# T's products behind Gram's, and the layer change's first transposes within the last products

## The chip, the cores and the metric

The kernel runs on one core of a Trainium2 chip. The metric is the device time of one execution in microseconds (us); lower is better. Times of several executions are given by their median. TensorE (PE) multiplies, VectorE (DVE) and ScalarE (ACT) work element by element, GpSimd (POOL) does the same and issues DMAs, SyncE (SP) issues DMAs.

## The reference

Two residual layers over 512 positions of 2048 channels. The first is gated differential attention with 8 heads, the second is gated RWKV-7 time mixing with 32 heads of 64 channels, whose state follows a generalised delta rule. Cut to what matters:

```python
x = x + out                                   # each layer: x <- x + W_out( mixer(rms_norm(x)) * silu(gate) )

# layer 0, per head: two softmaxes over 128 channels each, subtracted, times v
a = p[:, :, 0] - lam * p[:, :, 1]
o = rms_norm(a @ v, subln_w) * (1.0 - lambda_init) * silu(gate)

# layer 1: p = h @ w_in, mixed with the position before, split into r, k, v, g, dw, da
def step(S, inp):
    r_t, w_t, k_t, v_t, a_t, b_t = inp        # a = -kk, b = kk * iclr, kk = normalised k
    sa = jnp.einsum('bhvk,bhk->bhv', S, a_t)
    S = S * w_t[:, :, None, :] + sa[..., None] * b_t[:, :, None, :] + v_t[..., None] * k_t[:, :, None, :]
    y = jnp.einsum('bhvk,bhk->bhv', S, r_t)
    return S, y
```

## The kernel before

**Products and precision.** Each float32 operand is split into a rounded high part and the rest (`split_w` for weights: a copy on ScalarE, a subtraction on VectorE), and `mm3` (L114) makes three products of them. Nearly all products have 512 columns. `tick` counts these products: the kernel weaves small dependent work into the large products by hand. A `Chain` is a generator whose steps are issued on TensorE behind the large product at which its count of products runs out; each `yield n` asks for n more products before the next step. Only the first chain in the list counts down. `finish` issues what is left at once. Within this, the order of each engine's queue is fixed when the program is built, from priorities and modelled readiness; on the chip each queue runs in that order.

**Layer 0, attention.** While the large projections of head h run, a chain does the attention of head h - 1, in 4 blocks of rows: `scores`, `turn` (transposes of the weights a), `weigh` (product with v), and `turn_y` (L395: transposes of the result y into yT). `turn_y` uses PSUM tag pa, which has two banks and which `scores` uses too; `turn` uses pb, which has one. One pass of the loop is 40 products long, 21 for the last head, and between the first `yield 8` and the last one the block's weighing and scores are issued.

**Layer 0, end, and the change of layers.** The output product's second half of columns is done by `seven`, a scheme with seven products of blocks in place of eight. Its last part is product "22", summed into the banks z (tag pa) in three rounds of 12 products and added to x by `take("21", z)`. Behind `seven` stands the normalisation for layer 1: the sums of squares give rs for the first and the second 256 rows (rsqrt by 11 small steps on VectorE), `scale` multiplies x (L771), `half_h` transposes two column blocks of one half of the rows (L805, tag pa), `make_h` splits them into hH and hL, and the products named lora (L114) use these at once: 12 products of 256 columns for each pair of column blocks.

**Layer 1, the pairs.** 16 pairs of heads, j = 0 to 15. An iteration j has the large projections v of j, k of j + 1, the gate of j - 3, and r of j + 1, 48 products each (the gate from j = 3 on). Behind the 18th product of v the function `behind` is called:

- `gram` (L1065): 32 products of AR and BK of pair j into 4 banks gp; before the copies of their result (L1072) it takes one step of the chain of pair j - 1 (`before.step`). Then come the two sums (L984, L985), and the result is written to DRAM as ltd (L1084, on ScalarE's queue).
- `t_solve`: LT is loaded from ltd (L1118, POOL's queue), VectorE solves 31 dependent steps (L1129, L1131), and the result Tm goes to DRAM as td (L1133).
- `group_norm` of pair j - 2.

The chain of pair j - 1 is made at the start of iteration j, and its first step is taken there. In `t_combine` this step brings T in from td (L1146, SP's queue, four DMAs) and transposes it (L1155, T1, two transposes on VectorE, queued behind `g.centred`, the end of the centring of the pair before). After GAP_D products come T's first products (L1161, px, 32 small ones) with four copies (L1164, L1167); after GAP_X more its second ones (L1171) with two copies (L1174); after GAP_T more the scan: 8 chunks with three small dependent products each (L1242, L1253, L1260), 6, 6 and 8 products apart. At its end come the outputs Y (L1282, L1286) and their centring (L1297 to L1299).

With GAP_D = 18 the first products are issued at the 18th product of v by `tick`, just ahead of `behind`; the step that `gram` then takes is that of the second products. AR is made by `stage2` (L1049) at the start of iteration j on VectorE; r, from which it is made, is mixed there just before (L898).

Of the kernel before, what the change touches and what calls it, by code (L numbers as in the profile page):

```python
# [13 lines left out]
F32 = mybir.dt.float32  # L14
# [9 lines left out]
P = 128  # L24
# [3 lines left out]
NT = T // P  # L28
# [304 lines left out]
def attention(g, h, qkT, qkL, sq, V, VL, G, gap, rows=None):  # L333


    nc, w = g.nc, g.work
    yT = w.tile([P, 2, T], F32, name="yTh", tag="yTh", bufs=1)
    blocks = [Ctx() for _ in range(NT)]

    def scores(t):  # L340
        b, N = blocks[t], (t + 1) * P
        mx = g.small.tile([P, 2], F32, name="mx", tag="mx")
        nb = g.small.tile([P, 2], F32, name="nb", tag="nb")
        sm = g.small.tile([P, 2], F32, name="sm", tag="sm")
        pr = []
        for c in range(2):
            s = g.ps.tile([P, 512], F32, name="sc", tag="pa", bufs=2)
            ts = slice(t * P, (t + 1) * P)
            mm3(nc, s[:, :N], qkT[:, c, ts], qkL[:, c, ts], qkT[:, 2 + c, 0:N], qkL[:, 2 + c, 0:N], True, True)
            nc.vector.tensor_tensor_reduce(  # L350
                out=s[:, :N], in0=s[:, :N], in1=g.mask[:, (NT - 1 - t) * P :], scale=1.0, scalar=NEG,
                op0=ALU.add, op1=ALU.max, accum_out=mx[:, c : c + 1])
            nc.vector.scalar_tensor_tensor(nb[:, c : c + 1], mx[:, c : c + 1], -1.0, sq[:, t, c : c + 1],
                                           ALU.mult, ALU.mult)
            p_ = w.tile([P, 512], F32, name=f"p{c}", tag=f"p{c}", bufs=2)
            nc.scalar.activation(p_[:, :N], s[:, :N], AF.Exp, bias=nb[:, c : c + 1],
                                 scale=sq[:, t, c : c + 1], accum_out=sm[:, c : c + 1])
            pr.append(p_)
        b.r = g.small.tile([P, 2], F32, name="r", tag="r")
        nc.vector.reciprocal(b.r[:], sm[:])  # L360
        rho = g.small.tile([P, 1], F32, name="rho", tag="rho")
        nc.vector.scalar_tensor_tensor(rho[:], sm[:, 0:1], b.r[:, 1:2], g.neglam[:], ALU.mult, ALU.mult)
        b.a = w.tile([P, 512], F32, name="a", tag="a", bufs=2)
        nc.vector.scalar_tensor_tensor(b.a[:, :N], pr[1][:, :N], rho[:], pr[0][:, :N], ALU.mult, ALU.add)

    def turn(t):
        b, N = blocks[t], (t + 1) * P
        pt = g.ps.tile([P, 512], F32, name="pt", tag="pb")
        for i in range(t + 1):
# [4 lines left out]
        nc.vector.tensor_sub(b.al[:, :N], pt[:, :N], b.at[:, :N].bitcast(F32))  # L374

    def weigh(t):
        b = blocks[t]
        o = g.ps.tile([P, 512], F32, name="o", tag="pc")
        for i in range(t + 1):
            bs = slice(i * P, (i + 1) * P)  # L380
            mm3(nc, o[:, :256], b.at[:, bs], b.al[:, bs], V[:, i, :], VL[:, i, :], i == 0, i == t)
        junk = w.tile([P, 256], F32, name="junko", tag="junko", bufs=2)
        so = g.small.tile([P, 1], F32, name="so", tag="so")
        nc.scalar.activation(junk[:], o[:, :256], AF.Square, scale=b.r[:, 0:1], accum_out=so[:])
        nc.vector.tensor_scalar(so[:], so[:], 1.0 / 256, EPS, ALU.mult, ALU.add)
        ro = g.small.tile([P, 1], F32, name="ro", tag="ro")
# [3 lines left out]
        nc.vector.scalar_tensor_tensor(b.y[:], o[:, :256], ro[:], G[:, t, :], ALU.mult, ALU.mult)  # L390

    def turn_y(t):
        pt = g.ps.tile([P, 512], F32, name="yt", tag="pa", bufs=2)
        for i in range(2):
            nc.tensor.transpose(pt[:, i * P : (i + 1) * P], blocks[t].y[:, i * P : (i + 1) * P], g.ident[:])  # L395
        nc.scalar.copy(yT[:, :, t * P : (t + 1) * P], pt[:, :256].rearrange("p (c q) -> p c q", c=2))

    for i in range(NT + 3):
        if 0 < i <= NT:
            turn(i - 1)  # L400
        if i > 2:
            turn_y(i - 3)
        if i == NT + 2:
            break
        yield 8
        if 1 < i < NT + 2:
            weigh(i - 2)
        if i < NT:
            scores(i)
        yield gap - 8  # L410
    if rows is None:
        nc.scalar.dma_start(out=g.yd[h * 256 : (h + 1) * 256, :].rearrange("(c p) t -> p c t", p=P), in_=yT[:])
    else:
        rows += [split_row(g, yT[:, c, :]) for c in range(2)]
# [71 lines left out]
                          accum_op=ALU.add)  # L486


def seven(g, w, load, rows, sums, c1, c2, acc, Ts, banks, done):

# [35 lines left out]
    last = N - 1  # L526
# [36 lines left out]
    done("22")  # L563
    take("21", X)
    for i in range(N):
        prod(z, i, "22", Ts[i], i == 0, i == last)
    take("21", z)
    done("21")
# [16 lines left out]
def flat(t):  # L585

    n = "abc"[: len(t.shape) - 1]
    n = " ".join(n)
    return t[:].rearrange(f"p {n} -> p ({n})").rearrange("p (k c) -> p k c", k=KG)


def layer0(g, aps):
# [86 lines left out]
    with ExitStack() as cx:  # L679
# [50 lines left out]
        sums = []  # L730
# [27 lines left out]
        def banks(i):  # L758
            if i < 2:
# [6 lines left out]
        seven(g, aps["da_w_out"][0], load, rows, sums, 1024, 1536, acc, [flat(g.C), flat(g.S), T2], banks, done)  # L766

        rs = g.work.tile([P, NT], F32, name="rs1", tag="rs1", bufs=1)
        ss = g.work.tile([P, NT], F32, name="ss1", tag="ss1", bufs=1)
        def scale(cb, t):  # L770
            nc.vector.tensor_scalar(xs[cb][:, t, :], xs[cb][:, t, :], rs[:, t : t + 1], None, ALU.mult)  # L771

        for half in (slice(0, 2), slice(2, 4)):
            with tc.high_priority(offset=SOLVE if half.start else 0):
                nc.vector.reduce_sum(ss[:, half], g.ssx[:, half], AX.X)
                nc.vector.tensor_scalar(ss[:, half], ss[:, half], 1.0 / D, EPS, ALU.mult, ALU.add)
                rsqrt(g, rs[:, half], ss[:, half], 2, "r4")
                if half.start == 0:
                    for cb in range(4):
                        for t in range(2):  # L780
                            scale(cb, t)

        def more_h(n, m):
            for k in range(len(g.hH), min(n, KT)):
# [7 lines left out]
                with tc.high_priority(offset=AHEAD):  # L792
                    make_h(g, ps, KT + k)

        def half_h(k, half, m):

            ps = g.ps.tile([P, 512], F32, name="xT", tag="pa", bufs=2)
            for i in range(2):
                xq, c0 = xs[(k + i) // 4], (k + i) % 4 * P
                for t in range(2):  # L800
                    tt, at = 2 * half + t, (2 * i + t) * P
                    if c0 == 0 and half:
                        scale((k + i) // 4, tt)
                    with tc.issue_after(m.ins) if m else ExitStack():
                        nc.tensor.transpose(ps[:, at : at + P], xq[:, tt, c0 : c0 + P], g.ident[:])  # L805
            for i in range(2):
                with tc.high_priority(offset=AHEAD):
                    make_h(g, ps[:, 256 * i : 256 * i + 256], KT + k + i, k + i, half)

        pts = [g.ps.tile([P, 512], F32, name="lora", tag=tag) for tag in ("pb", "pc")]  # L810
        lora = [(aps["rw_w_in"][0], 4 * D, 2 * RK)]

# [5 lines left out]
            return m  # L818


        m, wts = None, []
# [312 lines left out]
    return ld.ins  # L1134


GAP_D, GAP_X, GAP_T = 18, 19, 8


def t_combine(g, j, p):  # L1140
# [370 lines left out]
```

## Time and profile before

| | |
|---|---|
| three timed runs | 2208.28, 2211.53, 2221.82 us, median 2211.53 |
| the profiled execution | 2206.95 us, span 2205.2 us, mean granted TensorE clock 0.993 |
| TensorE busy | 2171.5 us, 98% |
| VectorE, ScalarE, POOL busy | 1445.4, 1041.9 and 293.8 us |
| layer 0 | about 0 to 1000 us |
| layer 1 | about 1000 to 2205 us; one full iteration takes about 62 us |

A row of the timeline has the start in us from the span's start, the time in us (of several instructions together, if a count over 1 stands at its end), engine, line of the kernel, operation, the tiles written and read, and, in square brackets, how long the engine was idle before it and what ended that. A matmul's printed time includes its way through the array; the next one starts before it ends. The granted clock is a share of TensorE's full speed.

### The profile page before, as it was taken

To read this page: it belongs to the slowest core of one execution; us is meant where nothing else is said; L and a number is where in the kernel's file an instruction comes from. 1 tells how busy PE (TensorE), PEld (TensorE's weight loads), DVE (VectorE), ACT (ScalarE), POOL (GpSimd) and SP (SyncE) were. 2 spreads that over 40 slices of the span, in tenths; PEclk is the share of its full clock that TensorE was granted. 3 is DMA by queue.
4 is the path that set the end of the run, shared out by engine and by line. 5 is a ranking of instruction groups with operands and counts; after the bars stand their busy time and mean duration, and the time that the engine had idled before them with its cause. 6 is when DMAs were issued, how large, how long until landed. Compare 5 with 4: busy or idle time off the path is not lost.

```text
span 2205.2 us, 34098 instructions
## 1 busy us (share of the span) xinstructions
PE 2171.5 (98%) x12260; PEld 1767.9 (80%) x12260; DVE 1445.4 (66%) x3780; ACT 1041.9 (47%) x2118; POOL 293.8 (13%) x637
## 2 busy tenths in 40 slices
PE   9999999999999999999999999999999999999999
PEld 7888888888888888878777787878887788877887
DVE  5664646455654666475667877777778877767644
ACT  5443434334443454345455555555555556545322
POOL 0000000000000000110222222222222222221001
PEclk9999999999999999999999999999999999999999
DMA  6223222222323356653422333333333333446555
GB/s 192 96 79 98 84 96 96 86 96 87 96 77 99 131 171 225 158 117 90 106 57 76 81 87 86 93 97 92 91 87 85 96 91 77 113 123 187 172 167 119
DMA packets 296313, 240.20 MB, mean 109 GB/s; under 512 B 47792, under 2 KB 255680, under 8 KB 296144
## 3 DMA queue, kind: packets, MB, share of 16 engines
q1 hardware_dynamic: 256912, 190.13, 29.3%
q0 software_dynamic: 12384, 29.72, 6.3%
q10 hardware_dynamic: 26848, 18.18, 2.7%
q8 instruction: 96, 1.57, 0.3%
q14 instruction: 73, 0.60, 0.1%
HBM read 217.98 MB, written 19.99 MB: 108 GB/s over the span
## 4 chain that ended last, share of the span: by engine, by line
PE 70%; DVE 19%; issue 4%; DMA 3%; ACT 2%; SPq 0%; POOL 0%; ACTq 0%; DVEq 0%; POOLq 0%
PE pp L114 52%; PE pt L114 5%; DVE wl L103 3%; DVE tmpl L1129 3%; DVE Tm L1131 2%; DMA td<-Tm 2%; DVE VS L1264 1%; PE gp L1065 1%; PE sm L1242 1%; PE lora L114 1%; PE sc L114 1%; PE sm L1260 1%; DMA TT<-td 1%; ACT wh L102 1%; PE sm L1253 1%
## 5 line engine op out<-in xcount | busy, mean ns | idle before, releaser
L103 DVE TENSOR_TENSOR wl<-wraw,wh 128x1024 fp32r<-128x1024 f32 (+2 forms) x319 | 388.9, 1219 | 431.5 <-ACT wh L102 419.0
L102 ACT CAST wh<-wraw 128x1024 fp32r<-128x1024 f32 (+2 forms) x319 | 333.5, 1046 | 513.0 <-PE pp L114 378.3
L114 PE MATMUL pp<-wh,hH 128*128 128x512 f32 x1268 | 499.3, 394 | 0.3 <-DVE gs L326 0.2
L114 PE MATMUL pp<-wh,hL 128*128 128x512 f32 x1268 | 497.7, 393 | 0.1
L114 PE MATMUL pp<-wl,hH 128*128 128x512 f32 x1268 | 497.4, 392 | 0.0
L114 PE MATMUL pp<-hH,wl 128*128 128x512 f32 x1024 | 416.1, 406 | 0.3 <-DVE wl L103 0.3
L114 PE MATMUL pp<-hL,wh 128*128 128x512 f32 x1024 | 415.9, 406 | 0.0
L114 PE MATMUL pp<-hH,wh 128*128 128x512 f32 x1024 | 413.1, 403 | 0.0
L114 PEld LDWEIGHTS pp<-wh,hH 128*128 128x128 f32 x1268 | 238.3, 188 | 48.4 <-PE pp L114 0.6
L114 PEld LDWEIGHTS pp<-wh,hL 128*128 128x128 f32 x1268 | 238.3, 188 | 48.4 <-DVE hL L858 0.5
L114 PEld LDWEIGHTS pp<-wl,hH 128*128 128x128 f32 x1268 | 238.4, 188 | 46.4
L114 PEld LDWEIGHTS pp<-hH,wh 128*128 128x128 f32 x1024 | 194.6, 190 | 36.1 <-issue 0.9
L114 PEld LDWEIGHTS pp<-hL,wh 128*128 128x128 f32 x1024 | 194.6, 190 | 34.9
L114 PEld LDWEIGHTS pp<-hH,wl 128*128 128x128 f32 x1024 | 194.7, 190 | 32.9 <-DVE wl L103 0.7
L1129 DVE SCALAR_TENSOR_TENSOR tmpl<-LT,Tm 128x60 f32<-128x60 f32 (+24 forms) x496 | 135.1, 272 | 10.9
L1248 POOL COPY SA<-VS 64x64 f32<-64x64 f32 x224 | 60.9, 272 | 457.0 <-DVE VS L1264 350.0
L459 POOL DMA_DIRECT2D frow<-yd x12 | 8.9, 746 | 796.4 <-DVE rs_i L63 676.8
L1131 DVE TENSOR_TENSOR Tm<-Tm,tmpl 128x60 f32<-128x60 f32 (+24 forms) x496 | 104.0, 210 | 11.2
L1255 ACT COPY VS<-sm 64x64 f32<-64x64 f32 x256 | 52.9, 207 | 65.8 <-PE sm L1253 61.1
L1245 ACT COPY rhs<-sm 64x64 f32<-64x64 f32 x256 | 52.7, 206 | 53.7 <-PE sm L1242 51.3
L1264 DVE SCALAR_TENSOR_TENSOR VS<-sm,gam,Sg 64x64 f32<-64x64 f32 x192 | 54.1, 282 | 24.7 <-PE sm L1260 20.6
L1251 POOL TENSOR_SCALAR Sg<-SA,gam 128x64 f32<-128x64 f32 x96 | 63.3, 660 | 9.5 <-POOL SA L1248 0.2
(333 smaller groups left out, 3189.6 us busy)
## 6 DMA issues: line engine op xcount, KB each, us to landing
wraw<-in_rw_w_in_dram SPq DMA_DIRECT2D x128, 512.0 KB
wraw<-in_da_w_in_dram SPq DMA_DIRECT2D x254, 256.0 KB
wraw<-in_da_w_out_dram SPq DMA_DIRECT2D x26, 512.0 KB
wraw<-in_rw_w_out_dram SPq DMA_DIRECT2D x26, 512.0 KB
LT<-ltd POOLq DMA_DIRECT2D x64, 132.0 KB, 2.9
yr<-yd SPq DMA_DIRECT2D x28, 256.0 KB
frow<-yd POOLq DMA_DIRECT2D x12, 512.0 KB, 6.9
xq<-in_x_dram SPq DMA_DIRECT2D x16, 256.0 KB
```

The source lines that it names most:

```text
L102: nc.scalar.copy(hi[:, ks], raw[:, ks])
L103: nc.vector.tensor_sub(lo[:, ks], raw[:, ks], hi[:, ks].bitcast(F32))
L114: m = nc.tensor.matmul(out, a, b, start=s, stop=e, skip_group_check=skip)
L1065: m = nc.tensor.matmul(gp[h][:, i * P : (i + 1) * P], BK[r_, c0 + i, :, :], p.AR[r_, c0 + i, :, :], start=True, stop=True)
L1129: nc.vector.scalar_tensor_tensor(tt, LT[:, i : i + 1, i + 1 :].to_broadcast([P, s, n]), n2[:, i : i + 1], Tm[:, 0:s, i : i + 1].to_broadca ...
L1131: nc.vector.tensor_add(Tm[:, 0:s, i + 1 :], Tm[:, 0:s, i + 1 :], tt)
L1242: nc.tensor.matmul(sm[:, 0:P], both(p.G[:, c, 0]), both(VS[:, c]), start=True, stop=True)
L1245: nc.scalar.copy(rhs[r_, :], sm[r_, h * C : h * C + C])
L1248: nc.gpsimd.tensor_copy(p.SA[r_, c - 1, :], VS[r_, c, h, :])
L1251: nc.gpsimd.tensor_scalar(Sg[:], p.SA[:, c - 1, :], p.gam[:, c : c + 1], None, ALU.mult)
L1255: nc.scalar.copy(VS[r_, c, h, :], sm[r_, P : P + C])
L1264: g.state = nc.vector.scalar_tensor_tensor(VS[r_, c + 1, h, :], s_, p.gam[r_, c : c + 1], Sg[r_, :], ALU.mult, ALU.add)
```

## The change

It has three parts.

1. In `attention`, `turn_y` is issued 8 products later, behind `weigh` and ahead of `scores`, and takes bank pb in place of pa. The last block's `turn_y` stays at its place.
2. In the layer change, a new function `begin` is called by `seven` ahead of the last of the three rounds of product "22". It holds the normalisation of the first 256 rows, their first two scales, the transposes of the first four column blocks (two `half_h`, into banks of pool pp) with their `make_h`, and then the other six scales. The loop behind `seven` goes on from there.
3. In `t_combine`, GAP_D goes from 18 to 20 and GAP_X from 19 to 10. At the 18th product of v the first products' count is not yet out, so the step that `gram` takes is now that of the first products, and the second ones follow 10 products later.

```diff
     def turn_y(t):
-        pt = g.ps.tile([P, 512], F32, name="yt", tag="pa", bufs=2)
+        pt = g.ps.tile([P, 512], F32, name="yt", tag="pb")
...
         if 0 < i <= NT:
             turn(i - 1)
+        if i == NT + 2:
+            turn_y(i - 3)
+            break
+        yield 8
+        if i > 1:
+            weigh(i - 2)
         if i > 2:
             turn_y(i - 3)
-        if i == NT + 2:
-            break
-        yield 8
-        if 1 < i < NT + 2:
-            weigh(i - 2)
         if i < NT:
             scores(i)
         yield gap - 8
...
     for i in range(N):
+        if i == last and begin:
+            begin(g.m)
         prod(z, i, "22", Ts[i], i == 0, i == last)
     take("21", z)
...
+        def begin(m):
+            normalise(slice(0, 2))
+            for k in (0, 2):
+                half_h(k, 0, m, (g.pp, "pp", 4))
+            for cb in range(1, 4):
+                for t in range(2):
+                    scale(cb, t)
+
+        seven(g, aps["da_w_out"][0], load, rows, sums, 1024, 1536, acc, [flat(g.C), flat(g.S), T2], banks, done, begin)
+        normalise(slice(2, 4))
...
         for i, (k, half) in enumerate(turns):
-            if i == 0:
-                half_h(k, half, m)
-            if i + 1 < len(turns):
+            if 0 < i < len(turns) - 1:
                 half_h(*turns[i + 1], m)
-            else:
+            elif i:
                 more_h(KT // 2 + 1, m)
...
-GAP_D, GAP_X, GAP_T = 18, 19, 8
+GAP_D, GAP_X, GAP_T = 20, 10, 8
```

More of the change, by code (lines that the diff above doesn't have):

```diff
@@ L486, in add_w, with seven @@
                           accum_op=ALU.add)
-def seven(g, w, load, rows, sums, c1, c2, acc, Ts, banks, done):
+def seven(g, w, load, rows, sums, c1, c2, acc, Ts, banks, done, begin=None):
     nc = g.nc
@@ L765, in layer0 @@
                                               (g.work, "G", 1), (g.wraw, "wraw", 3)))
-        seven(g, aps["da_w_out"][0], load, rows, sums, 1024, 1536, acc, [flat(g.C), flat(g.S), T2], banks, done)
         rs = g.work.tile([P, NT], F32, name="rs1", tag="rs1", bufs=1)
@@ L771, in scale, with normalise @@
             nc.vector.tensor_scalar(xs[cb][:, t, :], xs[cb][:, t, :], rs[:, t : t + 1], None, ALU.mult)
-        for half in (slice(0, 2), slice(2, 4)):
+        def normalise(half):
             with tc.high_priority(offset=SOLVE if half.start else 0):
@@ L778, in layer0 @@
                 if half.start == 0:
-                    for cb in range(4):
-                        for t in range(2):
-                            scale(cb, t)
+                    for t in range(2):
+                        scale(0, t)
         def more_h(n, m):
@@ L793, in more_h, with half_h @@
                     make_h(g, ps, KT + k)
-        def half_h(k, half, m):
-            ps = g.ps.tile([P, 512], F32, name="xT", tag="pa", bufs=2)
+        def half_h(k, half, m, bank=(g.ps, "pa", 2)):
+            ps = bank[0].tile([P, 512], F32, name="xT", tag=bank[1], bufs=bank[2])
             for i in range(2):
@@ L808, in half_h @@
                     make_h(g, ps[:, 256 * i : 256 * i + 256], KT + k + i, k + i, half)
+        def begin(m):
[3 more added lines that the diff above has]
+            for cb in range(1, 4):
+                for t in range(2):
+                    scale(cb, t)
+        seven(g, aps["da_w_out"][0], load, rows, sums, 1024, 1536, acc, [flat(g.C), flat(g.S), T2], banks, done, begin)
+        normalise(slice(2, 4))
         pts = [g.ps.tile([P, 512], F32, name="lora", tag=tag) for tag in ("pb", "pc")]
@@ L818, in products @@
             return m
-        m, wts = None, []
+        m, wts = g.m, []
         turns = [(k, half) for half in range(2) for k in range(0, KT // 2, 2)]
         for i, (k, half) in enumerate(turns):
-            if i == 0:
-                half_h(k, half, m)
-            if i + 1 < len(turns):
+            if 0 < i < len(turns) - 1:
                 half_h(*turns[i + 1], m)
-            else:
+            elif i:
                 more_h(KT // 2 + 1, m)
```

## The prediction

> **What bounds the kernel now.** I read the page first, for the busy engine; then the waits of TensorE, for what still stops it; then, around each place that the diff touches, the timeline of the engines and the granted clock by stretches.
>
> ```profile
> span 2205.2 us, 34098 instructions
> PE 2171.5 (98%) x12260; PEld 1767.9 (80%) x12260; DVE 1445.4 (66%) x3780; ACT 1041.9 (47%) x2118; POOL 293.8 (13%) x637
> ...
> PE px L1161 <- DVE T L1155: 12.5, 13, 3.1
> ...
> PE yt L395 <- DVE y L390: 1.5, 8, 0.3
> ...
> PE lora L114 <- ACT hH L857: 1.1, 1, 1.1
> ```
>
> TensorE (PE) is busy 98% of the span. The columns of a wait are the time in all, how often, and the longest. The change takes no arithmetic away, so it can only win where TensorE stands still, and the three waits shown are those that its three parts touch: T's first products (px, L1161), the transposes of y (yt, L395) and the first products of the second layer (lora). The same question asked of 1260 to 1940 us alone, where the pairs of heads run at full pace, shows how little of the first is left there:
>
> ```profile
> PE px L1161 <- DVE T L1155: 3.2, 7, 1.0
> ```
>
> Of the 12.5 us, 7.8 us are thus outside, mostly in the first three chains, where T is late for another reason (below).
>
> **Second layer, T's products.** Here is TensorE around a pair whose T was in time, and around one whose T was late:
>
> ```profile
> 1391.66 1.09 PE L1161 MATMUL px<-T,G 32*32 32x32 f32 x32
> 1392.68 2.06 PE L1065 MATMUL gp<-AR,BK 64*128 64x128 f32 x32
> 1394.67 1.09 PE L1171 MATMUL px<-TT,X 32*32 32x32 f32 x32
> 1395.69 0.40 PE L984 MATMUL pt<-sHx,ones 128*2 128x512 f32 x1
> 1395.93 0.40 PE L985 MATMUL pt<-sLx,ones 128*2 128x512 f32 x1
> ...
> 1452.87 0.69 PE L1161 MATMUL px<-T,G 32*32 32x32 f32 x16
> 1453.92 0.69 PE L1161 MATMUL px<-T,G 32*32 32x32 f32 x16 [0.36 <-DVE T L1155]
> 1457.55 0.40 PE L984 MATMUL pt<-sHx,ones 128*2 128x512 f32 x1
> ```
>
> A product of 512 columns takes 0.23 to 0.24 us from start to start (1395.69 to 1395.93), and the kernel's gaps count such products. The order is T's first products (1.0 us), Gram (2.0), T's second products (1.0). In time, the group takes 1395.69 - 1391.66 = 4.03 us; with T late it takes 1457.55 - 1452.87 = 4.68. So a wait printed as 0.36 costs 0.65: 0.29 is hidden in the modelled end of the matmul before. The seven waits of 3.2 us are worth 3.2 + 7 x 0.29 = 5.2 us, which is all that the steady pairs can give.
>
> Why is T late? VectorE's queue for the late pair:
>
> ```profile
> 1447.45 0.75 DVE L1299 TENSOR_TENSOR yc<-Y,s 128x256 f32<-128x256 f32 x2
> 1449.62 1.23 DVE L103 TENSOR_TENSOR wl<-wraw,wh 128x1024 fp32r<-128x1024 f32 x1 [1.43 <-ACT wh L102]
> 1450.77 0.74 DVE L898 SCALAR_TENSOR_TENSOR mixr<-pp,prmin_rw_mu_dram,mixr 128x511 f32<-128x511 f32 x1
> 1452.38 0.44 DVE L1155 STREAM_TRANSPOSE T<-TT 64x256 f32<-64x256 f32 x1 [0.87 <-DMA TT<-td]
> 1452.75 0.64 DVE L1049 TENSOR_TENSOR AR<-mixr,E 128x512 f32<-128x512 f32 x1
> 1453.43 0.44 DVE L1155 STREAM_TRANSPOSE T<-TT 64x256 f32<-64x256 f32 x1
> ```
>
> The first transpose of T waits for the DMA that brings TT, and AR, which Gram reads, stands behind it. AR ends at 1453.39, 0.52 us after the group began. **This is the point on which the change turns**: Gram is first now, and if that queue stayed as it is, Gram would wait for AR where T's products waited before: it would begin near 1453.45, and 4.03 us on is 1457.48 instead of 1457.55. That bound is a gain of 0.1 us a pair, next to nothing.
>
> But the queue does not stay as it is, since T itself comes earlier. The Gram values leave through ScalarE and a chain of DMAs before the next T can be solved:
>
> ```profile
> 1394.42 2.06 ACT L1072 COPY G<-gp 128x512 f32<-128x512 f32 x4
> ...
> 1402.12 0.31 ACTq L1084 DMA_DIRECT2D ltd<-G  x1
> ```
>
> Gram began at 1392.68 and its copies started only at 1394.42, after T's own copies. With Gram first it begins 1.0 us earlier, and its first half can be copied after 1.0 us, while ScalarE still has nothing from T to copy: the copies move from 2.8 us after the group's start (1394.42 - 1391.66) to some 1.0, thus 1.8 us earlier. ScalarE's last issue of ltd (1402.12) stands in its queue behind the copies of the scan, and POOL's loads of LT behind that. The scan begins ten products (2.3 us) later, so these issues get ahead of it: 2 to 4 us earlier for LT, and so for T, of the next pair, against a lateness of about 1 us. The second T products, ten products on, no longer stand directly behind Gram: they start 3.0 + 0.5 (the two sums) + 2.3 = 5.8 us after Gram's start. Gram's copies would end at 1.0 + 2.06 and T's four copies, which fill 1392.75 (the end of px) to 1394.42, need 1.7 more: 4.8 us, in time. The scan ends ten products later too: Y's centring (L1297 to L1299), behind which T's transposes are queued, would be ready 2.3 us later; VectorE has the 1.43 us of idle time before wl to take it up, and an earlier end of the solve in front of it. Issued instructions and DMAs stay the same in number; on SP the four TT loads keep their place, and the weight loads behind them wait less if td comes earlier. From 0.1 x 7 = 0.7 to 5.2 us I take **4.0**, nearer the upper end, because the shift (2 to 4 us) is larger than the lateness.
>
> The last pair in this order is a case of its own:
>
> ```profile
> 1946.32 0.69 PE L1161 MATMUL px<-T,G 32*32 32x32 f32 x16 [0.46 <-DVE T L1155]
> 1947.67 0.48 PE L1065 MATMUL gp<-AR,BK 64*128 64x128 f32 x2 [0.67 <-DVE AR L1049]
> ...
> 1940.00:1960.00 20.00, 18.86 (x151) 0.83 0.33 88
> ...
> 1148.83 0.69 PE L1161 MATMUL px<-T,G 32*32 32x32 f32 x16 [1.83 <-DVE T L1155]
> ...
> 1140.00:1160.00 20.00, 18.16 (x139) 0.77 0.28 58
> ...
> 1700.17 0.69 PE L1161 MATMUL px<-T,G 32*32 32x32 f32 x16 [0.97 <-DVE T L1155]
> ...
> 1700.00:1720.00 20.00, 19.33 (x172) 1.00 0.45 115
> ```
>
> (In a row by stretches, the clock stands behind the count.) Here 1.13 us of idle time, among small products, were followed by a lower clock: (1 - 0.83) x 20 = 3.4 us lost. The same follows the 1.83 us at 1148.83 (0.77), and not the 0.97 us at 1700.17. With T in time the idle time goes and, I think, the low clock with it: 0 to 1.1 + 3.4 = 4.5; I take **4.0**. [...]
>
> The first three chains (1148.83 is one) get little: T's products were placed well after Gram there, since T came later still. Zero, with ±3 us for the phase of their clock. The last chain gains by place: its start moves 10 + 2 products (2.8 us) later while its T does not.
>
> ```profile
> 2013.38 0.69 PE L1161 MATMUL px<-T,G 32*32 32x32 f32 x16 [0.43 <-DVE T L1155]
> ...
> 2015.09 0.69 PE L1161 MATMUL px<-T,G 32*32 32x32 f32 x16 [0.58 <-DVE T L1155]
> ```
>
> That is 0 to 1.0; I take **1.0**.
>
> **Layer change.** Before, the first transposes wait until the last sum has left its two banks:
>
> ```profile
> 979.44 0.39 PE L114 MATMUL z<-wh,hL 128*128 128x512 f32 x1
> 980.00 1.25 PE L805 MATMUL xT<-ident,xq 128*128 128x128 f32 x8 [0.18 <-DVE xq L523]
> 982.34 0.47 PE L114 MATMUL lora<-hH,wh 128*96 128x256 f32 x2 [1.08 <-ACT hH L857]
> 984.78 0.60 PE L805 MATMUL xT<-ident,xq 128*128 128x128 f32 x4
> 985.13 0.36 PE L114 MATMUL lora<-hH,wh 128*96 128x256 f32 x1
> ...
> 985.60 0.48 DVE L771 TENSOR_SCALAR xq<-xq,rs 128x512 f32<-128x512 f32 x1
> ```
>
> From the end of z's issue (979.67) to the next four transposes (984.78) pass 5.1 us. The work in it is 8 transposes at 0.09 (four take 984.78 to 985.13) and 12 products of 256 columns at half of 0.23, together 2.1 us, 2.3 with a little for the changeover. So 2.8 us are idle. The change puts the transposes before z's last 12 products, into banks of another pool: the sum's way out, hH and hL are then covered by 12 x 0.23 = 2.8 us of products. What is late next is the second half's scale: ready at 985.60 + 0.48, or 6.4 us after z; it will be wanted after 36 products and 8 transposes, 4.9 us after z, and the hL subtractions that stand between its small steps now are done before. That leaves 0 to 1.5 us late; I count 0.3 of it. Bounds 0 (the cover fails) to 2.8; I take **2.5**. If scale or hL were late before z's last products, TensorE would wait there instead; the first half's scales follow sums that left long before z's.
>
> **First layer, y.** The transposes of y move 8 products and one weighing later, and into bank pb.
>
> ```profile
> 258.50 0.68 DVE L374 TENSOR_TENSOR al<-pt,at 128x512 fp32r<-128x512 f32 x1
> ...
> 260.05 0.28 PE L114 MATMUL o<-V,al 128*128 128x256 f32 x1
> ...
> 268.90 0.44 PE L395 MATMUL yt<-ident,y 128*128 128x128 f32 x2 [0.17 <-DVE y L390]
> ```
>
> 1.8 us more (8 x 0.23) hides waits of 0.17 here and at most 0.3 (the row of waits above). Bank pb is free in time: al, its last reader, ends at 259.18, and the weighing ends at 260.17. The last transposes of a head stay where they were. Of 1.5 us printed plus hidden tails of about 0.15 each, I take **2.0** (bounds: a loss of 1 if pb blocks, a gain of 2.5).
>
> **Sum.** 4.0 + 4.0 + 1.0 + 2.5 + 2.0 = 13.5, less 2.0 for new small waits (AR behind T in a few pairs, X's copies): 11.5 us. The profiled execution took 2206.95 us, its span 2205.2, so it would become 2195.5. The three timed runs before have a median of 2211.53, 4.6 above it, and such a median is what will be read: 2211.5 - 11.5 = **2200 us**. One per cent is 22 us, about what a measurement of this kernel can tell from no change; this is half of it.
>
> **Rivals.**
> 1. *The wait moves to AR.* VectorE's queue keeps T before AR, T gains nothing, Gram waits. For: that order in the rows of 1452. Against: the copies are freed 1.8 us earlier. Steady pairs 0.7, last pair 0; left are 1.0 + 2.5 + 2.0: 2211.5 - 6 = 2205. Chance 0.2.
> 2. *Slower: both transposes of T get ahead of AR.* The scan's ten products push the centring, T's transposes follow it, and AR comes behind both. In the pair of 1452, T from 1452.38, twice 0.44 and AR's 0.64 end at 1453.9: Gram begins 1.05 us late, the group ends at 1457.95, 0.4 later than now. Over 11 pairs that is 5 us. It decides when Gram's idle time passes the 1.13 us that were followed by a low clock in the last pair: 3.4 us in every second of 11 pairs is 19 more. 2211.5 + 24 - 5.5 = 2230; with every fourth, 2220. I put it at 2224. Chance 0.1.
> 3. *The low clock of the last pair stays*, being due to the small products and not to the idle time: 2200 + 3.4 = 2203. [...] Chance 0.1.
> 4. *The layer change does not do what it says*: the transposes wait before the last products for their scale. Its 2.5 us are lost: 2203. For: scale and hL share VectorE with the last wl. Against: the first scales ran well ahead of z's end. Chance 0.1.
>
> **How the numbers follow.** Forecast 0.5, rivals 0.2, 0.1, 0.1 and 0.1. The likeliest case reaches from 2191 (all upper bounds and no dip) to 2208; rivals 1, 3 and 4 lie in it. To take in the unknown phase of the first three chains' clock and the edge of rival 2, the range goes up to 2216. Faster by over 1% (below 2189.4) needs the dips of the first chains to vanish as well: 0.06. Slower by over 1% (above 2233.6) is rival 2 at its worst: 0.05. Within 1%: 0.89.
>
> **What would show it.** Right: Gram's 32 products first, T's 32 behind them without a wait, a group of 3.0 us up to the sums; Gram's copies begin about 1 us after Gram; the waits of px on T fall from 12.5 to near 8, all in the first three chains; clock 1.00 in the last pair; lora without a wait on hH; yt's waits near 0.3. Wrong: a new wait of gp on AR in most pairs (rival 1 or 2), new stretches of low clock after 1260 us, or xT waiting on L771.

## The result and the profile after

The changed kernel takes 2230.3 us in the median (2227.3 to 2234.2, 7 runs); the kernel before, run beside it, 2208.3 (2200.4 to 2221.8). The ratio is 1.009, with a 95% interval of [1.0063, 1.0117]. That is about 0.9% slower, and it lies above the range of the prediction. The profiled execution took 2234.22 us.

The span, the busy time and the waits of TensorE, and the mean granted clock, from the page and from the views of waits and of cores of the changed kernel (lines of layer 1 stand 10 further on):

```profile
span 2232.5 us, 34031 instructions
...
PE 2183.4 (98%) x12260; PEld 1780.1 (80%) x12260; DVE 1448.0 (65%) x3780; ACT 1045.9 (47%) x2118; POOL 280.7 (13%) x637
...
PE px L1171 <- DVE T L1165: 21.6, 13, 3.1
PE sm L1252 <- DVE VS L1274: 10.6, 14, 0.9
PE px L1171 <- DVE y L1333: 1.9, 1, 1.9
...
PE gp L1075 <- DVE AR L1059: 1.0, 2, 0.6
...
core 0: 2232.5 us, clock 0.986
```

The kernel before has this in place of the second wait:

```profile
PE sm L1242 <- DVE VS L1264: 3.0, 13, 0.3
```

The wait for T, which was to fall from 12.5 to 8 us, has risen to 21.6. A new one stands behind it: the scan's first product of a step (sm) waits for its state VS, 10.6 us against 3.0. As an estimate from the mean clock, (1 - 0.986) x 2232.5 = 31 us went to a lower clock, against 15 before (0.993). Gram hardly waits for AR. The first large product of the second layer now starts at 1010.30, 2.6 us earlier than before (1012.90), so all of the loss is in the second layer: from there to the end of the span pass 2232.5 - 1010.3 = 1222.2 us, against 2205.2 - 1012.9 = 1192.3.

Here is a pair of the changed kernel, on TensorE, VectorE, ScalarE and POOL:

```profile
1389.17 2.06 PE L1075 MATMUL gp<-AR,BK 64*128 64x128 f32 x32
1392.44 0.69 PE L1171 MATMUL px<-T,G 32*32 32x32 f32 x16 [1.21 <-DVE T L1165]
...
1393.61 0.69 PE L1171 MATMUL px<-T,G 32*32 32x32 f32 x16
1398.30 1.09 PE L1181 MATMUL px<-TT,X 32*32 32x32 f32 x32
...
1388.43 0.69 DVE L1059 TENSOR_TENSOR AR<-mixr,E 128x512 f32<-128x512 f32 x1
...
1391.95 0.91 DVE L1165 STREAM_TRANSPOSE T<-TT 64x256 f32<-64x256 f32 x2 [2.04 <-DMA TT<-td]
...
1390.37 1.56 ACT L1082 COPY G<-gp 128x512 f32<-128x512 f32 x3 [3.78 <-PE gp L1075]
1393.16 0.62 ACT L1177 COPY G<-AR 64x512 f32<-64x512 f32 x1 [1.23 <-PE px L1171]
...
1395.74 0.59 ACT L1082 COPY G<-gp 128x512 f32<-128x512 f32 x1
...
1399.43 0.36 ACT L1184 COPY TT<-px 32x256 f32<-32x256 f32 x1 [1.56 <-PE px L1181]
1399.65 0.62 ACTq L1088 DMA_DIRECT2D ltd<-ssl  x1
...
1403.25 0.21 ACT L1265 COPY VS<-sm 64x64 f32<-64x64 f32 x1 [1.14 <-PE sm L1263]
1403.26 0.31 ACTq L1094 DMA_DIRECT2D ltd<-G  x1
...
1405.36 0.31 ACTq L1094 DMA_DIRECT2D ltd<-G  x1
...
1407.51 2.04 POOL L1128 DMA_DIRECT2D LT<-ltd  x4 [1.07 <-DMA ltd<-G]
```

Gram comes first and in time, as the change wants it. But ScalarE, after three of Gram's four copies, turns to T's copies and waits 1.23 us for px, which itself waits for T. The fourth Gram copy comes at 1395.74, the first ltd behind the copy to TT that had to wait 1.56 us for T's second products, and the last two behind a copy of the scan (VS) that had waited 1.14 us: 1405.36, 16.2 us after Gram, against 9.4 in the pair shown of before. LT is loaded 18.3 us after Gram. A late T thus delays the input of the next T. The pair is typical: in the ten pairs in a row whose T is late (Gram from 1326.18 to 1908.26) the last ltd goes out 14.3 to 19.4 us after Gram and LT is loaded 16.5 to 21.7 us after it; in the pairs of before from 1331.65 to 1885.72 it was 9.4, and 12.2 to 14.0. ScalarE kept the order of its queue even where it stood idle: by its row Gram was done at 1389.17 + 2.06 = 1391.23, ahead of the 1.23 us of idle time that end at 1393.16, and still its fourth copy came behind T's.

The clock in two stretches with such a pair and, in the last row, with the last chain. From 1260 us on, every stretch of 20 us was at 1.00 before, except that of the last pair:

```profile
1380.00:1400.00 20.00, 18.72 (x204) 0.91 0.39 94
...
1640.00:1660.00 20.00, 16.86 (x163) 0.85 0.39 93
2040.00:2060.00 20.00, 17.94 (x118) 0.74 0.60 179
```

### The profile page after: what moved, and what is told of

Read it like the earlier page. It is cut to its first block, busy times and chain, and to the rows that moved or that the text cites. A ratio compares the mean times of both kernels' runs of the same rounds, so it can differ in the third digit from the quotient of the medians.

```text
span 2232.5 us, 34031 instructions
## 1 busy us (share of the span) xinstructions
PE 2183.4 (98%) x12260; PEld 1780.1 (80%) x12260; DVE 1448.0 (65%) x3780; ACT 1045.9 (47%) x2118; POOL 280.7 (13%) x637
## 4 chain that ended last, share of the span: by engine, by line
PE 71%; DVE 18%; DMA 5%; issue 4%; ACT 2%; POOL 0%; SPq 0%; ACTq 0%; DVEq 0%; POOLq 0%
PE pp L114 54%; PE pt L114 5%; DVE tmpl L1139 4%; DVE Tm L1141 3%; DMA td<-Tm 2%; DVE wl L103 2%; DMA TT<-td 2%; PE sc L114 1%; DVE VS L1274 1%; PE o L114 1%; PE px L1171 1%; PE sm L1252 1%; PE px L1181 1%; PE sm L1270 1%; DVE l L1024 1%
## 5 line engine op out<-in xcount | busy, mean ns | idle before, releaser
L103 DVE TENSOR_TENSOR wl<-wraw,wh 128x1024 fp32r<-128x1024 f32 (+2 forms) x319 | 394.1, 1235 | 402.1 <-ACT wh L102 397.2
L114 PE MATMUL pp<-hH,wl 128*128 128x512 f32 x1024 | 421.8, 412 | 0.3 <-DVE wl L103 0.3
L114 PE MATMUL pp<-hL,wh 128*128 128x512 f32 x1024 | 421.3, 411 | 0.0
L114 PE MATMUL pp<-hH,wh 128*128 128x512 f32 x1024 | 420.4, 411 | 0.0
L1252 PEld LDWEIGHTS sm<-VS,G 128*128 128x128 f32 x256 | 45.3, 190 | 31.1 <-PE pp L114 19.0
```

Of the source, the lines that this page charges most:

```text
L103: nc.vector.tensor_sub(lo[:, ks], raw[:, ks], hi[:, ks].bitcast(F32))
L114: m = nc.tensor.matmul(out, a, b, start=s, stop=e, skip_group_check=skip)
L1252: nc.tensor.matmul(sm[:, 0:P], both(p.G[:, c, 0]), both(VS[:, c]), start=True, stop=True)
```

## The experiments

### Which part loses

gaps_only is the kernel before with the two numbers; attention_only and change_only are the kernel before with one of the other two edits; no_gaps has both of these and the old numbers.

```diff
-GAP_D, GAP_X, GAP_T = 18, 19, 8
+GAP_D, GAP_X, GAP_T = 20, 10, 8     # gaps_only: this alone
```

> The kernel before with GAP_D, GAP_X = 20, 10 alone. If the loss comes whole from T's products (theory F, feedback: ScalarE's fourth Gram copy and the issues of ltd stand behind copies that wait for T, so a late T makes the next T late): 22 to 28 us slower than before, ratio 1.010 to 1.013, with waits of px on T of about 20 us and a last issue of ltd 14 to 19 us after Gram's start in the steady pairs. If the three parts act on each other instead (the layer change shifts the phase of the pairs): under 10 us slower.

> The kernel before with the first layer's turn_y behind the weighing and in bank pb, alone. Prediction's term: 2.0 us faster, from the trace of the changed kernel 1.8 us, seen as an earlier start of the last z products; ratio 0.999, not to be told from no change in the times. Rival (pb blocks the transposes): new waits of yt on al, 0 to 1 us slower.

> The kernel before with the layer change's part alone. The prediction's 2.5 us would show as 36.0 us from z's last group to the second layer's first large product; if the second half's scale has become the bound, as the trace of the changed kernel suggests, it stays at 38.4 us. Time: 0 to 2.5 us faster, ratio 0.999 to 1.000.

> The changed kernel with its old gaps (18, 19, 8) put back, so that only the edits in attention and at the layer change remain. If all of the loss sits in the three numbers of the gaps, as the runs so far say, this kernel beats both: ratio to the kernel before 0.994 to 0.997 (attention alone gave 0.9957, the layer change alone 0.9982), about 2200 us. If the three edits disturb each other (a shift of phase in the second layer), it is 0.999 or above.

Measured: gaps_only 1.007 [1.0043, 1.0098], attention_only 0.9957 [0.9933, 0.9981], change_only 0.9982 [0.9958, 1.0006], no_gaps 0.9972 [0.9955, 0.9988] (2205.3 us). The loss is all in the two numbers: 2230.3 - 2205.3 = 25 us. The version without them beats both kernels. By themselves the two numbers cost less than I had expected, 15 us (0.007 x 2212) and not 22 to 28; why they cost some 10 us more beside the other two edits is not shown, and part of it may be noise, as the intervals reach 4 to 6 us to either side. In gaps_only the same two waits stand as in the changed kernel (px on T 18.4 us, sm on VS 10.3). attention_only is better than expected, 9.5 us in the ratio; its profiled span is only 3.2 us shorter than that of before (2202.0), 2.6 us of it in the first layer (the z product that starts at 974.50 before starts at 971.86), so the rest is not accounted for.

### The order in ScalarE's queue

In the changed kernel `gram` takes T's step before its own copies. ltd_first takes it behind Gram's copies and the issues of ltd, copies_first between the two.

```diff
-    if before:
-        with g.tc.issue_after(m.ins):
-            before.step(g)
     ...                                   # Gram's four copies
+    if before:                            # copies_first: here
     ...                                   # the sums, ssl, the issues of ltd
+    if before:                            # ltd_first: here
+        with g.tc.issue_after(m.ins), g.tc.issue_after(ld.ins):
+            before.step(g)
```

> The changed kernel with one edit in gram: the chain's step is taken after Gram's copies and the issues of ltd, and its ScalarE copies are queued behind these. Theory F: the last issue of ltd comes within 10 us of Gram's start (14 to 19 in the changed kernel), T is in time from the second steady pair on, waits of px on T fall from 21.6 to under 9 us, all in the first three chains, no low clock after 1260 us: 2195 to 2210 us. Rival S (the scan, ten products later, collides with VectorE's other work and makes the solve longer): the scan stays where it is, so it stays at 2225 to 2235 us.

> The changed kernel, but T's step is taken up only behind Gram's four copies in ScalarE's queue (not behind the ltd issues, as in ltd_first). The gaps stay 20, 10, 8. Theory: most of the feedback goes (px on T 7 to 12 us instead of 21.6), since the fourth Gram copy no longer waits for px; the later scan stays (sm on VS near 10 us): ratio 1.002 to 1.005. If the ltd issues behind T's copies are what matters, px on T stays at 15 to 21 and the ratio at 1.007 to 1.009.

ltd_first: 1.0024 [1.0004, 1.0044], 2216.7 us. copies_first: 1.0098 [1.0075, 1.0122]; its rival was right, and the wait for T is nearly that of the changed kernel:

```profile
PE px L1171 <- DVE T L1165: 20.0, 14, 2.9
```

The waits and the clock of ltd_first:

```profile
PE sm L1252 <- DVE VS L1274: 10.7, 15, 1.0
PE px L1171 <- DVE T L1165: 7.7, 3, 3.1
PE gp L1075 <- DVE AR L1059: 5.5, 7, 1.5
...
core 0: 2213.1 us, clock 0.996
```

The waits for T outside the first three chains are gone, and the clock is up from 0.986. What fed the late T back are the issues of ltd behind T's copies, not Gram's copies: in copies_first Gram's copies no longer stand behind T's, but LT is still loaded 16.7 to 21.1 us after Gram in the ten pairs from 1320.76 to 1900.51; in ltd_first it is loaded 11.1 to 11.6 us after it (1326.25 to 1893.29). That is 2230.3 - 2216.7 = 14 of the 25 us. The remaining 11 us were not expected there (2195 to 2210 was), and the scan's waits are as long as before.

scan_back is copies_first, and order_only the kernel before, with numbers that put Gram first but start the scan where it was:

```diff
+GAP_D, GAP_X, GAP_T = 20, 6, 2
```

> The kernel copies_first with the gaps 20, 6, 2 in place of 20, 10, 8: T's second products follow 6 products behind the first and the scan 2 behind those, so the scan starts where it did before the change, with Gram ahead of T's products and T's copies behind Gram's. Theory: both mechanisms are gone. sm on VS falls to about 3 us, px on T to 7 to 8 (the first three chains alone), the dips of the clock between 1260 and 2020 us go, and with the gains of attention and of the layer change the ratio is 0.992 to 0.997. If the start of the scan doesn't matter, it is that of copies_first, 1.002 to 1.005, with sm on VS near 10. New risk: px waits for X (its copies stand behind Gram's four), up to 0.5 us a pair, 5 us in all, which would give 0.997 to 0.999.

> The kernel before with the gaps 20, 6, 2: Gram goes ahead of T's first products, while T's second products and the scan start where they did (no edit in attention or at the layer change). Theory: the order feeds itself by ScalarE's queue even with the scan in place, because T's copies, the scan's first rhs copies and VS copies stand ahead of the last ltd issues: px on T 15 to 30 us, ltd issued 12 to 21 us after Gram, ratio 1.005 to 1.025. Rival: the loss comes from the later scan alone and the order is harmless: ratio 0.999 to 1.002, px on T near 12.

scan_back 1.0273 [1.0249, 1.0298], order_only 1.0318 [1.0285, 1.035]. My expectation for scan_back was wrong by the most. The waits, and a pair on ScalarE and POOL, of order_only (its Gram begins at 1744.75):

```profile
PE px L1161 <- DVE T L1155: 31.1, 15, 3.6
...
PE sm L1242 <- DVE VS L1264: 2.9, 13, 0.3
...
1759.89 0.20 ACT L1255 COPY VS<-sm 64x64 f32<-64x64 f32 x1 [1.10 <-PE sm L1253]
1759.96 0.62 ACTq L1078 DMA_DIRECT2D ltd<-ssl  x1
...
1765.72 0.31 ACTq L1084 DMA_DIRECT2D ltd<-G  x1
...
1769.35 2.03 POOL L1118 DMA_DIRECT2D LT<-ltd  x4 [0.35 <-issue]
```

With the scan in its old place, its copies come ahead of ltd: even the first half of ssl is sent behind a VS copy, the last ltd goes out 21.0 us after Gram, and LT is loaded at 24.6. The scan's own waits are back at 2.9 us. So the later start of the scan does let the ltd issues pass, as the prediction had it; but it only softens a harm that Gram's place ahead of T brings, and it has a price of its own.

### The later scan by itself

distance_only leaves T's first products ahead of Gram and only lets the second ones follow by count, so that the scan starts ten products later. scan_later delays the scan alone.

```diff
-GAP_D, GAP_X, GAP_T = 18, 19, 8
+GAP_D, GAP_X, GAP_T = 18, 10, 8          # distance_only
-                    gram(g, j, p, j > 1 and pairs[j - 1].chain)
+                    gram(g, j, p, None)  # distance_only
+GAP_D, GAP_X, GAP_T = 18, 19, 18         # scan_later
```

> The kernel before with one thing of the gaps alone: T's first products stay ahead of Gram, but the second ones are no longer pulled directly behind it; they follow ten products after the first by the gap, so the scan starts about ten products later. Theory (two mechanisms: T's copies ahead of Gram's copies and ltd issues feed a late T back to itself; and the later scan meets VectorE's queue): px on T waits little more than the 12.5 us of before, since Gram's copies are again delayed only by T's first copies, while sm waits on VS about 0.8 us a pair (10 us in all): ratio 1.003 to 1.007. If the order ahead of Gram is all that matters, ratio 0.999 to 1.001 and sm on VS stays near 3. If distance alone is all, ratio 1.007 to 1.010, as with the whole gaps.

> The kernel before with one number changed: the gap ahead of the scan is 18 products in place of 8. T's first and second products stay around Gram as before; only the scan starts ten products later. Theory: the later start by itself costs, since the scan's steps now meet VectorE's and ScalarE's weight casts (wl 1.2 us, wh 1.05 us) in another phase: sm waits on VS for 10 us and more in all instead of 3, ratio 1.005 to 1.010, like distance_only. Rival: in distance_only it was the place of T's second products (their copies to TT stand among the ltd issues); then this kernel is within 0.999 to 1.002 and sm on VS stays below 5 us.

distance_only: 1.0094 [1.0075, 1.0113], at the clock of before, 0.993; that is not what my theory gave, but the outcome named for the case that the distance alone is all. scan_later: 1.0121 [1.0106, 1.0136]; there the chain before ends so late that, only the first chain in the list counting, Gram gets ahead of T's products too, and Gram's own wait for the centring (yc, 20.0 us in 11) comes on top. distance_only is the clean one of the two. Its waits, the place of one of them, and POOL in the pair whose Gram begins at 1719.88:

```profile
PE sm L1242 <- DVE VS L1264: 13.2, 22, 1.0
PE sm L1260 <- ACT VS L1255: 9.7, 16, 0.7
...
1767.47 0.46 PE L1242 MATMUL sm<-VS,G 128*128 128x128 f32 x2 [0.97 <-DVE VS L1264]
...
1765.18 1.22 DVE L103 TENSOR_TENSOR wl<-wraw,wh 128x1024 fp32r<-128x1024 f32 x1
1766.56 0.28 DVE L1264 SCALAR_TENSOR_TENSOR VS<-sm,gam,Sg 64x64 f32<-64x64 f32 x1
...
1733.66 0.45 POOL L1251 TENSOR_SCALAR Sg<-SA,gam 128x64 f32<-128x64 f32 x1
1734.44 2.04 POOL L1118 DMA_DIRECT2D LT<-ltd  x4 [0.34 <-issue]
```

The scan's steps wait 22.9 us for VS, where it was 3.8 before (3.0 and 0.8); the 19.1 us more are most of the 22.2 us that the span is longer. The new VS stands behind a weight's subtraction (wl, 1.2 us) on VectorE, or behind the weight's copy (wh, 1.03 us, as at 1756.91, ahead of a step that waits 0.72 us) on ScalarE. POOL, moreover, issues the loads of LT at 14.6 us after Gram, right behind the scan's first Sg, which the later scan has delayed; in the pair of before whose Gram begins at 1701.85 they went out at 1714.11, 12.3 after, 1.8 us behind that Sg, when a DMA of ltd had landed.

### What the later scan runs into

Three tries to take that away: the weight casts in two halves (distance_halves), the loads of LT from SyncE's queue (distance_sp), both (halves_sp).

```diff
-    for ks in [slice(k, k + 1) for k in range(kg)] if fine else [slice(0, kg)]:
+    for ks in [slice(k, k + s) for s in [1 if fine else 4 if kg == 8 else kg] for k in range(0, kg, s)]:
...
-        ld = nc.gpsimd.dma_start(out=LT[i * 32 : i * 32 + 32], ...
+        ld = nc.sync.dma_start(out=LT[i * 32 : i * 32 + 32], ...
```

> distance_only (1.0094) with each weight cast of a projection in the second layer in two halves, of four rows of tiles each, on ScalarE (wh) and on VectorE (wl): a scan step that comes up behind a cast waits for half of it at most. Some 0.06 us more of fixed cost for each instruction. Theory (the scan stands behind a cast): the waits of sm on VS, 13.2 us from VectorE and 9.7 us from ScalarE, fall to half or less, and the ratio to 1.002 to 1.006. Rival (the waits come from the chain of small steps itself, or from queues in which the casts are not the cause): they stay above 18 us in all, ratio 1.008 to 1.011.

> distance_only (1.0094) with the loads of LT issued from SyncE's queue. There TensorE waited for the scan's own steps (23 us) and for T only in the first chains (7.3 us). Theory: T comes earlier and nothing follows from it, ratio 1.007 to 1.010, sm on VS still 18 us or more. Rival (a late solve is what puts the scan's steps out of phase): sm on VS falls below 12 and the ratio below 1.005.

> distance_halves (1.0114) with the four loads of LT issued from SyncE's queue in place of GpSimd's, where they stand behind the scan's first copies to SA. Theory (GpSimd's queue makes T late once the scan starts later): LT is loaded 0.5 to 1.5 us earlier in each pair, px on T falls from 24.1 us (21 waits) to 8 to 14, ratio 1.004 to 1.008. Rival (T is late because the ltd issues themselves are late in ScalarE's queue, behind the scan's copies): LT waits for ltd instead, px on T stays above 18, ratio 1.010 to 1.013.

distance_halves 1.0114 [1.0097, 1.0131], distance_sp 1.0078 [1.0052, 1.0103], halves_sp 1.0097 [1.0069, 1.0126]. The waits of distance_halves:

```profile
PE px L1161 <- DVE T L1155: 24.1, 21, 6.0
PE sm L1260 <- ACT VS L1255: 10.4, 15, 0.8
...
PE sm L1242 <- DVE VS L1264: 0.8, 4, 0.3
```

Halving wl took the waits for VectorE's VS away, 13.2 to 0.8 us, so the cast was what VS stood behind there. The waits for ScalarE's VS did not fall (9.7 before the halving): there both halves of wh still stand ahead of VS, as at 1440.44, 1.12 us together. No time came of it, since T became late instead; why it did is not shown. LT from SyncE does not cure that (halves_sp: LT 13.6 us after the Gram of 1407.53, against 14.9 after that of 1403.15 in distance_halves, and still 27.6 us for T); the theory of GpSimd's queue fell. distance_sp stayed slower, as expected there, though its waits for VS (16.9 us in all) are shorter than I had said. VectorE's rows of the kernel before show the 0.06 us that each further instruction was expected to cost: an operation on 1024 columns takes 1.14 us from start to start (2089.59 to 2090.73), one on 512 takes 0.60 (2090.73 to 2091.33), and 2 x 0.60 - 1.14 = 0.06.

The same halves in ltd_first, and ltd_first with the scan up to six products earlier (gaps 20, 10, 2):

> ltd_first (the changed kernel with T's step behind the ltd issues; 1.0024) with each weight cast of a projection in the second layer in two halves. There T was in time with some 2 us to spare, and sm waited on VS for 10.7 us behind wl. Theory: the VS waits fall below 3 us and T stays in time, ratio 0.996 to 1.000, within 0.002 of the kernel with no new gaps (0.9972). Rival (as in distance_halves, another wait takes the place of the one removed): ratio 1.002 to 1.008, with a new wait of 8 us or more in the list.

> ltd_first (1.0024) with one number changed: the gap between T's second products and the scan is 2 in place of 8, so the scan starts up to six products (1.4 us) earlier; Gram first, ltd issued ahead of T's copies. Theory (it is the scan's place that costs what is left): sm on VS falls from 10.7 us to 3 to 6, ratio 0.998 to 1.001. Rival (what is left is the order's own cost: Gram waiting for AR, 5.5 us, and X copied late): sm on VS and the ratio stay, 1.002 to 1.004. Third: T's last copies to TT are not done for the first step, and sm waits for them or for rhs, 0.5 us a pair: 1.004 to 1.007.

ltd_first_halves 1.0084 [1.0056, 1.0112], ltd_first_t2 1.0183 [1.0157, 1.021]: the theory missed in both; for ltd_first_halves it came out about as its rival had it. The wait for VectorE's VS fell in both (5.7 and 0.7 us), and in both another one took its place. Of ltd_first_t2:

```profile
PE gp L1075 <- DVE AR L1059: 24.0, 13, 3.3
...
1459.38 0.44 DVE L1165 STREAM_TRANSPOSE T<-TT 64x256 f32<-64x256 f32 x1 [1.50 <-DMA TT<-td]
...
1460.48 0.69 DVE L1059 TENSOR_TENSOR AR<-mixr,E 128x512 f32<-128x512 f32 x1
```

Here T's transpose, waiting for its DMA, stands ahead of AR, and Gram waits for AR. That is the queue of my rivals 1 and 2. It is real, but in these kernels and not in the changed one, where AR is ahead (1388.43 against 1391.95). Each of these edits moves the queues of all engines when the program is built, so none of them takes away just one wait. The last 11 us of ltd_first are waits and not the clock, which is 0.996 in no_gaps too: beside no_gaps, ltd_first waits 7.6 us more for VectorE's VS, 1.9 for ScalarE's, 4.2 for AR and 2.8 in the last chain, and 5.9 less for T, 10.6 us of the 13.9 us by which its span is longer. Whether one of them can go without another taking its place stays open.

### The layer change

half1_early works the second half's scale out from the first half's sums, and leaves the second half's own out.

```diff
-                nc.vector.reduce_sum(ss[:, half], g.ssx[:, half], AX.X)
+                nc.vector.reduce_sum(ss[:, half], g.ssx[:, 0:2], AX.X)
```

> The changed kernel, but the scale of the second half at the layer change is worked out from the sums of the first half (the second half's own sums of squares are left out of it), so that it does not have to wait for z's squares. Looked at: the time from the first z product of the last rounds to the first large product of the second layer (38.40 us before, 38.36 after). Theory: the chain from z over the squares, the sum and the ten small steps of the reciprocal root has become what the second half waits for: without it the stretch is 36.5 to 37.5 us. Rival: the time goes to the transposes among the last z products and to hL behind wl in VectorE's queue: 38.0 to 38.5.

The rows of the changed kernel, and then those of half1_early:

```profile
971.94 0.50 PE L114 MATMUL z<-wl,hH 128*128 128x512 f32 x1 [0.24 <-DVE wl L103]
...
975.23 0.44 PE L806 MATMUL xT<-ident,xq 128*128 128x128 f32 x2 [0.45 <-DVE xq L773]
...
978.57 0.39 PE L114 MATMUL z<-wh,hL 128*128 128x512 f32 x1
978.80 0.28 PE L114 MATMUL lora<-hH,wh 128*96 128x256 f32 x1
...
1010.30 0.39 PE L114 MATMUL pp<-hL,wh 128*128 128x512 f32 x1
...
984.86 0.88 DVE L773 TENSOR_SCALAR xq<-xq,rs 128x512 f32<-128x512 f32 x2
```

```profile
972.48 0.50 PE L114 MATMUL z<-wl,hH 128*128 128x512 f32 x1 [0.27 <-DVE wl L103]
...
1009.73 0.39 PE L114 MATMUL pp<-hL,wh 128*128 128x512 f32 x1
```

From the first of these z products to the first large product of the second layer pass 1010.30 - 971.94 = 38.36 us; before it were 38.40 (974.50 to 1012.90), in change_only 38.38. In half1_early it is 37.25. So the gap between z and lora did close (2.9 us from start to start before, 0.23 now), while z itself ends 1.7 us later: 0.45 of waiting for scale, 0.82 for the eight transposes (975.23 to 975.42 and 976.01 to 976.64, up to the start of the next product), and the other 0.4, as an estimate, for the changes to and from them. At the next four transposes the changed kernel is 2.0 us ahead: they start 980.21 - 971.94 = 8.27 us after that z product, where it was 984.78 - 974.50 = 10.28. Behind them all of it is lost again. half1_early gives 1.1 us back, so about that much goes to the second half's scale, which starts 6.3 us after z's last product (984.86 - 978.57; 6.2 before, 985.60 - 979.44), and z's last product now comes later. The other 0.9 us are not accounted for. The gain is zero.

## Why the prediction was wrong

- **The term for T's products in the steady pairs** (+4.0) is where it failed. It rested on "while ScalarE still has nothing from T to copy", and on the ltd issues getting "ahead of" the scan. I let Gram's copies start 1 us after Gram, which three of them do (1390.37), and took the rest of the queue to follow. But the queue is fixed: one Gram copy and all ltd issues stand behind T's copies, and a late T holds them. Before, T's products stood ahead of Gram, so a late T delayed TensorE once, and Gram's copies found T's already done. In place of LT 2 to 4 us earlier, the pair shown has it 6.0 us later (18.3 after Gram against 12.3). Between 1260 and 1940 us, where the printed wait for T was to go from 3.2 us to none, it rose to 14.9. ltd_first shows what the queue is worth: 14 us.
- **The scan's ten products** I costed at the centring alone. Their price is in the scan's own steps, 3.0 to 10.6 us of waits for VS; distance_only shows 1.0094 from the distance with the old order. The small waits of 2.0 that I set against the gain named AR and X, neither of which counted.
- **The low clock**: right for the last pair, wrong for the others, where the working had no dip. With T later, dips came into eight of the pairs from 1326 to 1908 us, some 16 us by the stretches of 20 us. In ltd_first, with T in time, the clock is 0.996. The working also read too much into 1.13 us with a dip and 0.97 without: the pair at 1700.17 has a second wait of 0.38 us at 1701.24, 1.35 us in all, and no dip.
- **The last pair and the last chain** (+4.0, +1.0): in the last pair (Gram at 1973.14) T is in time, Gram waits 0.38 us for AR, and the clock from 1940 to 2000 us is 1.00, so its term came as forecast. The last chain took it back: it now waits 1.9 us for y (L1333), and at 0.74 from 2040 to 2060 us it loses (1 - 0.74) x 20 = 5.2 us. Together nothing was gained.
- **The layer change** (+2.5): the cover worked and the gain was zero. I named the second half's scale as late next and counted 0.3; what the cover gains (2.0 us up to the second group of transposes) is lost again behind it, 1.1 us to that scale and 0.9 unexplained. I had also taken the transposes to cost no more inside z than behind it; inside it they cost 0.82 us and that 0.4.
- **Attention's y** (+2.0): right. yt's waits fell from 1.5 to 0.2 us in all, and the first layer of attention_only is 2.6 us shorter; its whole time fell by more (9.5 us), which this does not explain.
- **The rivals**: the slower one came near the time (2224) and had the low clock in many pairs, but not the mechanism, so that is luck. Its chance was given to AR behind T in VectorE's queue; the order that decided was ScalarE's.
- **A slip without weight**: of the 12.5 us of waiting for T, 12.5 - 3.2 = 9.3 lie outside 1260 to 1940 us, not 7.8; 7.8 are those of the first three chains, the other 1.5 those of the last pair and the last chain.

## What to carry to other kernels

When a step is moved, write out the fixed order of every engine's queue behind it, and ask for each instruction there whether it now waits for something later than before; above all for DMA issues that feed the next round of the same loop. A loop whose result comes just in time (T one microsecond late of 62) has no room for that, so a delay comes back each round. Moving small dependent work to fill one gap shifts it against everything else in the period: measure the shift alone before counting the gap.

## What the runs showed of the hardware

Idle time alone does not set the clock in these runs. The changed kernel dips to 0.91 with 1.21 us of idle time between Gram and T's 32x32 products (1389.17 to 1393.61). ltd_first_t2 keeps 1.00 with nearly twice as much, ahead of Gram and behind large products:

```profile
1396.88 2.06 PE L1075 MATMUL gp<-AR,BK 64*128 64x128 f32 x32 [2.21 <-DVE AR L1059]
...
1380.00:1400.00 20.00, 17.79 (x183) 1.00 0.43 111
```

The stretch behind it, 1400 to 1420 us, is at 1.00 too. Nor is it the kind of products beside the wait alone: in the changed kernel, between Gram and the same 32x32 products, 1.19 us at 1329.42 left the clock at 1.00, and 1.04 us at 1782.01 came with 0.91. What else sets the clock is not shown here; no run varied the size of these products or the time at which the wait falls.
